# The product of the merged branches as seven products of quarters

## The chip, the cores and the metric

The kernel runs on one core of a Trainium2 chip. The metric is the device time of one launch in microseconds (us), as the median of several runs. Engines are named as the profile names them: PE is TensorE (PEld its weight loads), DVE VectorE, ACT ScalarE, POOL GpSimd, SP the engine that issues most transfers.

## What is computed

Two blocks of a model follow each other on 512 tokens of width 1024, in float32. The change is in the first one:

```python
gates = jax.nn.sigmoid((u @ w_gate[l] + b_gate[l]).astype(jnp.float32)).astype(u.dtype)
g_ssm, g_attn = jnp.split(gates, 2, axis=-1)
merged = g_ssm * (y_ssm @ w_up_ssm[l]) + g_attn * (y_attn @ w_up_attn[l])
h = h + merged @ w_out[l]
hid = jax.nn.relu(rmsnorm(h, norm_mlp[l]) @ w_ff1[l])
h = h + (hid * hid) @ w_ff2[l]
```

`y_ssm` and `y_attn` have width 512, `merged` and `w_out` 1024, `w_ff1` is 1024 x 4096. The product at issue is `merged @ w_out[l]`, 512 x 1024 by 1024 x 1024. Before it stand the two up-projections, behind it the norm and the feed-forward products.

## The kernel before

Every product of float32 numbers is made of three matmuls: both sides are split into a high part and a rest (`split`, L281: ACT copies to the rounded type, DVE subtracts it from the source), and `mm3` (L289) adds high by high, high by low and low by high. Weights come in chunks of 128 x 1024 (0.5 MB). A plan, the list that `order` (L1897) makes, gives their sequence: `load` (L317) fetches a chunk on SP's queue, `chunk_split` (L333) splits it on ACT and DVE, and at most four split pairs live at a time (`PAIRS`); `done` (L352) frees a pair once its matmuls are written down.

The feed-forward products are made already by seven products of quarters in place of eight (`seven_cm` and `seven`, L417; the names P1 to P7 and their sequence in `SEVEN`, L28). Their weight sides are sums of quarters: in `SUMS` (L30) a chunk is either loaded, or a transfer on POOL's queue adds the next quarter to a buffer that holds the one before (`accum_op`, L330). Results of P1, P2 and so on are added to `h` or subtracted from it as they come (`seven_h`, L463). Between P5 and P3 the same PSUM bank goes on being summed, so DVE must have read it in between. `Sides` (L110) holds the seven left sides.

Writing the program down, `Net` keeps an estimated clock: side tasks (`spawn`, L179) are put in between the matmuls when their inputs are thought to be ready (`wait`, `when`, L167), and `until` (L205) goes on when a condition holds. A scheduler then fixes the order on each engine, and each engine works off its own list in that order.

In `first` (L1035) the up-projection of the attention branch (L1217) goes over eight blocks m of 128 columns: 12 matmuls, DVE's product with the gate `gt[m, 1]`, POOL's addition of the other branch (`ptt`, L790), and the split into `mg`, a pair of 128 x 8 x 512. The four loads of `h` follow (`open_h`), since `h` takes the place of the gates. `tm_add` (L1239) makes `merged @ w_out` in two halves of 512 columns: for the first half six of eight steps in k for all four row tiles, and then the last two steps; for the second half tile by tile, and behind each tile `norm_sides` (L528) is spawned, the norm, the transposes by PE and the sides of the first feed-forward product. `ff` (L1267) starts its P1 once the tiles 0 and 1 are through, and P5 once 2 and 3 are.

## Time and profile before

| | |
|---|---|
| time, median of 3 runs | 1383.54 us (1383.09 to 1384.86) |
| the profiled execution | 1383.01 us, span 1381.3 us |
| busy: PE, DVE, ACT, POOL | 1346.5, 966.2, 725.2, 213.0 us |
| mean granted clock of PE | 0.995 |
| up-projections end, out-projection begins | 330.1 us |
| first feed-forward matmul | 378.7 us |

The profile is of one execution; its times count from the span's start. Matmuls are pipelined, so the time from one start to the next is what one costs, not its shown duration. A row of the timeline gives start, duration, engine, line, operation, the tile written and those read, and in brackets the engine's idle time before it and what ended that. Most operations have line L73, the helper that records them; so they are told apart by their tiles.

### The profile page before, as it was taken

How to read it: one execution, taken by the hardware profiler on the slowest of the kernel's cores; microseconds unless marked ns; L12 is line 12 of the kernel's file. 1: busy time of each engine (PE TensorE's matmuls, PEld its weight loads, DVE VectorE, ACT ScalarE, POOL GpSimd, SP SyncE). 2: the span in 40 equal slices, each digit the busy share in tenths (PEclk: the TensorE clock that was granted, in tenths of full speed). 3: DMA queues.
4: the chain of work that ended last, by engine and by line, in shares of the span. 5: the costliest groups of instructions: out<-in, count | busy, mean ns of one | idle time of the engine just before them, and what ended most of it. 6: DMA issues, size and time to landing. Idle time of an engine off the chain costs nothing. (4 is left out here: it accounts for less than half of the span.)

```text
span 1381.3 us, 20776 instructions
## 1 busy us (share of the span) xinstructions
PE 1346.5 (97%) x7914; PEld 1125.3 (81%) x7914; DVE 966.2 (70%) x1795; ACT 725.2 (52%) x1215; POOL 213.0 (15%) x248
## 2 busy tenths in 40 slices
PE   8989999999999999999989999999999999999997
PEld 7778886778798998979867776788898989898886
DVE  8987548874588677686883646544668887878555
ACT  6244347742476574746575422324546675756353
POOL 3155214224011111111210011000000000000000
PEclk9989999999999999999999999999999999999999
DMA  7444331113387778878721311322432222222422
GB/s 276 133 131 133 92 107 47 61 62 107 153 198 163 186 181 202 187 174 204 175 75 61 122 65 41 105 86 92 139 109 85 92 77 77 78 76 70 168 92 76
DMA packets 56883, 164.32 MB, mean 119 GB/s; under 512 B 14048, under 2 KB 15200, under 8 KB 56784
## 3 DMA queue, kind: packets, MB, share of 16 engines
q1 hardware_dynamic: 47568, 129.43, 27.3%
q0 software_dynamic: 9216, 33.56, 13.4%
q8 instruction: 63, 1.03, 0.3%
q14 instruction: 36, 0.29, 0.1%
HBM read 156.15 MB, written 6.82 MB: 118 GB/s over the span
## 5 line engine op out<-in xcount | busy, mean ns | idle before, releaser
L223 PE MATMUL bank<-w_hi,x_h 128*128 128x256 f32 (+1 forms) x744 | 257.3, 346 | 0.0
L223 PE MATMUL bank<-x_h,w_hi 128*128 128x512 f32 (+1 forms) x704 | 249.5, 355 | 7.3 <-ACT w_hi L73 5.3
L223 PE MATMUL bank<-w_hi,x_l 128*128 128x256 f32 (+1 forms) x744 | 248.8, 335 | 1.3 <-DVE x_l L73 1.3
L73 DVE TENSOR_TENSOR w_lo<-w_raw,w_hi 128x1024 fp32r<-128x1024 f32 (+1 forms) x160 | 195.0, 1224 | 76.6 <-ACT w_hi L73 76.0
L223 PE MATMUL bank<-w_lo,x_h 128*128 128x256 f32 (+1 forms) x744 | 248.6, 334 | 0.0
L223 PE MATMUL bank<-x_h,w_lo 128*128 128x512 f32 (+1 forms) x704 | 244.5, 347 | 0.0
L223 PE MATMUL bank<-x_l,w_hi 128*128 128x512 f32 (+1 forms) x704 | 244.4, 347 | 0.0
L73 ACT ACTIVATE w_hi<-w_raw 128x1024 fp32r<-128x1024 f32 (+1 forms) x162 | 167.1, 1035 | 126.4 <-PE bank L223 99.7
L223 PEld LDWEIGHTS bank<-w_hi,x_h 128*128 128x128 f32 x744 | 140.2, 189 | 20.7 <-issue 6.9
L223 PEld LDWEIGHTS bank<-x_h,w_hi 128*128 128x128 f32 x704 | 134.3, 191 | 24.9 <-ACT w_hi L73 5.3
L223 PEld LDWEIGHTS bank<-w_hi,x_l 128*128 128x128 f32 x744 | 140.1, 188 | 16.8 <-DVE x_l L73 1.8
L223 PEld LDWEIGHTS bank<-w_lo,x_h 128*128 128x128 f32 x744 | 140.5, 189 | 14.0 <-issue 0.3
L223 PEld LDWEIGHTS bank<-x_h,w_lo 128*128 128x128 f32 x704 | 134.1, 191 | 16.6 <-DVE w_lo L73 0.2
L223 PEld LDWEIGHTS bank<-x_l,w_hi 128*128 128x128 f32 x704 | 134.4, 191 | 14.9 <-DVE x_l L73 0.5
L73 DVE TENSOR_TENSOR w_lo<-w_a,w_hi 128x1024 fp32r<-128x1024 f32 x64 | 77.4, 1222 | 31.2 <-ACT w_hi L73 31.0
L73 ACT ACTIVATE w_hi<-w_a 128x1024 fp32r<-128x1024 f32 x64 | 67.7, 1060 | 59.9 <-PE bank L223 30.6
L73 POOL DMA_DIRECT2D w_a<-in_w_ff_dram x48 | 41.7, 874 | 220.8 <-DVE w_lo L73 204.4
L73 POOL TENSOR_TENSOR r<-v,pw 128x1 f32<-128x1 f32 x40 | 24.1, 604 | 299.3 <-DVE v L73 296.5
L73 DVE TENSOR_TENSOR h<-h,bank 128x512 f32<-128x512 f32 x80 | 54.4, 682 | 18.3 <-PE bank L223 15.1
L73 ACT ACTIVATE w_hi<-w_b 128x1024 fp32r<-128x1024 f32 x32 | 34.0, 1061 | 45.2 <-PE bank L223 39.3
L73 DVE TENSOR_TENSOR w_lo<-w_b,w_hi 128x1024 fp32r<-128x1024 f32 x32 | 38.6, 1222 | 16.2 <-ACT w_hi L73 16.2
L73 POOL TENSOR_TENSOR kn<-kn,gn 128x256 f32<-128x256 f32 x16 | 12.9, 809 | 237.7 <-ACT q L73 129.0
(427 smaller groups left out, 2798.3 us busy)
## 6 DMA issues: line engine op xcount, KB each, us to landing
w_a<-in_w_ff_dram POOLq DMA_DIRECT2D x48, 512.0 KB, 5.6
w_raw<-in_w_g_dram SPq DMA_DIRECT2D x16, 512.0 KB, 3.7
w_a<-in_w_ff_dram SPq DMA_DIRECT2D x16, 512.0 KB, 4.2
w_b<-in_w_ff_dram SPq DMA_DIRECT2D x16, 512.0 KB, 4.8
w_raw<-in_w_ff_dram SPq DMA_DIRECT2D x16, 512.0 KB, 4.7
w_b<-in_w_ff_dram POOLq DMA_DIRECT2D x16, 512.0 KB, 6.0
w_raw<-in_ple_gate_dram SPq DMA_DIRECT2D x16, 512.0 KB, 3.6
w_raw<-in_f_qk_dram SPq DMA_DIRECT2D x16, 512.0 KB, 3.5
```

The lines of the kernel that those rows point to most:

```text
L73: r = f(*args, **kw)
L223: self.nc.tensor.matmul(out, lhs, rhs, start=start, stop=stop, skip_group_check=more)
```

## The change

- The plan lists `w_out` as seven products: 14 chunks, eight loaded and six added by POOL's transfers, in place of eight. For that `wx`, the pool of the buffers `w_a` and `w_b`, is opened before the up-projection, not after it.
- `mg` becomes a pair of 128 x 7 x 4 x 256: the sides of the seven products, by k block and token half. For blocks 0 to 3 the first half is split at once for P1, and one difference is formed. For blocks 4 to 7 a task, `merged_sides`, forms the other sides from the block and its partner of four before: it splits both halves (P2 and P4), makes three sums and differences of 256 elements, and splits four sides at once (128 x 4 x 256).
- `tm_add` is not called here; `seven` is, with `evac` that updates `h` and spawns `norm_sides` for tiles 0 and 1 behind P6, and for 2 and 3 behind P4. From P2 on all four tasks must have been written down.
- Three of the side pairs of the feed-forward product get their memory only after the out-projection.

```diff
--- before.py
+++ after.py
@@ -323,7 +323,7 @@
         (buf, i), chunk, how = part
         if how == "load":
             tag, bufs = ("w_raw", self.RAW) if buf == "c" else (f"w_{buf}", 2)
-            t = self.parts[buf, i] = (self.wp if buf == "c" else self.wx.pool).tile([P, WC], F32, name=tag, tag=tag, bufs=bufs)
+            t = self.parts[buf, i] = (self.wp if buf == "c" else self.wx).tile([P, WC], F32, name=tag, tag=tag, bufs=bufs)
             self.nc.sync.dma_start(t, self.ins[name][chunk])
         else:
             t = self.parts[buf, i]
@@ -552,6 +552,7 @@
                 nc.scalar.activation(a21, b, AF.Copy)
             else:
                 v.tensor_tensor(s1, b, a21, ALU.subtract)
+                yield lambda: len(sides.pairs) == 7
                 self.split(*[cut(t) for t in sides["P5"]], s1)
                 sides.a22.append((tt, b))
             yield 0
@@ -1206,14 +1207,14 @@
         vx.close()
         yx.close()
         cx = ExitStack()
+        self.wx = self.pool(cx, "wx")
+        self.feed()
         pe = self.pool(cx, "pe")
-        ext = [[pe.tile([P, D], F32R, name=f"x{i}{s}") for s in "hl"] for i in range(3)]
-        xf = [t.rearrange("p k t -> p (k t)") for t in self.x]
-        sides = Sides([[t[:, i * D:i * D + D] for t in xf] for i in range(4)] + ext)
         ez = lambda: pe.tile([P, 4, 256], F32, name="z", tag="z", bufs=4)
-        z = [ez() for _ in range(4)]
         mx = ExitStack()
-        mg = self.pair(self.pool(mx, "mg"), 8, "mg")
+        pm = self.pool(mx, "mg")
+        mg = [pm.tile([P, 7, 4, 256], F32R, name=f"mg{s}") for s in "hl"]
+        up, self.merged, zs = slice(0, 256), 0, []
         for m in range(8):
             if m % 2 == 0:
                 w = self.weights("w_upa", m // 2, 8)
@@ -1223,18 +1224,51 @@
             g = self.gt[m, 1]
             nc.vector.tensor_tensor(g, g, b, ALU.mult)
             self.ptt(g, g, self.gt[m, 0], ALU.add)
-            self.split(mg[0][:, m], mg[1][:, m], g)
+            if m < 4:
+                zs.append(ez())
+                self.split(mg[0][:, 0, m], mg[1][:, 0, m], g[:, up])
+                nc.vector.tensor_tensor(zs[m][:, 0], g[:, up], g[:, 256:], ALU.subtract)
+            else:
+                self.spawn(self.merged_sides(mg, m - 4, g, self.gt[m - 4, 1], zs[m - 4]))
         px.close()
         self.open_h(ins["x"])
-        self.wx = ExitStack()
-        self.wx.pool = self.pool(self.wx, "wx", side="right")
+        xf = [t.rearrange("p k t -> p (k t)") for t in self.x]
+        sides = Sides([[t[:, i * D:i * D + D] for t in xf] for i in range(4)])
+        z = [ez() for _ in range(4)]
         tx = ExitStack()
         pn = self.pool(tx, "pn", side="right")
         g = self.row(pn, "norm_mlp")
 
         self.hold = self.plan.index(next(c for c in self.plan if c[:2] == ("w_ff1", (0, "P5", 0))))
-        th = self.tm_add(mg, "w_out", 0, lambda tt: self.norm_sides(pn, sides, z, self.h[tt], tt, g), mid=lambda: None)
-        self.ff(th, tx, mx, cx, sides, z, ez)
+        th = {}
+
+        def evac(p, s, b):
+            self.seven_h(p, s, b)
+            if p in ("P6", "P4"):
+                tt = s if p == "P6" else 2 + s
+                th[tt] = self.spawn(self.norm_sides(pn, sides, z, self.h[tt], tt, g))
+
+        self.seven("w_out", 0, lambda p, s, k: [t[:, LEFT[p], k, s * P:s * P + P] for t in mg], evac,
+                   lambda p: self.until(lambda: p == "P1" or self.merged == 4))
+        mx.close()
+        px = self.pool(cx, "ext")
+        sides.pairs += [[px.tile([P, 4, 256], F32R, name=f"x{i}{s}") for s in "hl"] for i in range(3)]
+        self.ff([th[tt] for tt in range(NT)], tx, cx, sides, z, ez)
+
+    def merged_sides(self, mg, k, g, g0, z):
+
+        v = self.nc.vector
+        up, lo = slice(0, 256), slice(256, 512)
+        s2, s1, s4 = (z[:, LEFT[p] - 3] for p in ("P6", "P5", "P3"))
+        yield self.when(g)
+        self.split(*[t[:, 1:3, k] for t in mg], g.rearrange("p (a t) -> p a t", a=2))
+        v.tensor_tensor(s1, g[:, lo], g0[:, lo], ALU.subtract)
+        v.scalar_tensor_tensor(s2, s1, -1.0, g0[:, up], ALU.mult, ALU.subtract)
+        v.scalar_tensor_tensor(s4, s2, -1.0, g[:, up], ALU.mult, ALU.subtract)
+        yield self.when(z)
+        self.split(*[t[:, 3:7, k] for t in mg], z)
+        self.merged += 1
+        yield self.wait()
 
     def tm_add(self, x, name, idx, then, before=None, mid=None):
 
@@ -1264,10 +1298,9 @@
         hs = self.h[tt][:, cb * 512:cb * 512 + 512]
         self.nc.vector.tensor_tensor(hs, hs, b, ALU.add)
 
-    def ff(self, th, tx, mx, cx, sides, xz, ez):
+    def ff(self, th, tx, cx, sides, xz, ez):
         nc = self.nc
         v = nc.vector
-        mx.close()
         hx = ExitStack()
         slots = lambda name, n: [[t.tile([P, 4, 256], F32R, name=f"{name}{i}{s}") for s in "hl"]
                                  for t in [self.pool(hx, name)] for i in range(n)]
@@ -1365,7 +1398,6 @@
                     norms[2 + s] = self.spawn(self.two_norms(ez, self.x, 2 + s, *z["g"]))
 
             self.seven("w_ff2", q * 8, lambda p, s, k: [t[:, k, s * P:s * P + P] for t in hid[p]], evac, first)
-        self.wx.close()
         hx.close()
         self.gla(norms, cx)
 
@@ -1905,7 +1937,6 @@
         add("w_qk", *range(8))
         add("w_ups", *range(4))
         add("w_upa", *range(4))
-        add("w_out", *range(8))
 
         def seven(name, base):
             for pr in SEVEN:
@@ -1913,6 +1944,7 @@
                 for i in range(2):
                     p.append((name, (base, pr, i), ((buf, i), base + 4 * c + 2 * k + i, how)))
 
+        seven("w_out", 0)
         for q in range(4):
             seven("w_ff1", 8 * q)
             seven("w_ff2", 8 * q)
```

The order of the instructions moves most on DVE. The first place is the end of the up-projection, from the split of block 5 to the split of block 7 (`gt51`, `gt61`, `gt71` are the gates of blocks 5 to 7, `mg_l` or `mgl` the low sides, `z` the sums and differences). DVE before:

```order
L73 TENSOR_TENSOR mg_l_3142<-gt51_546,mg_h_3141 128x512
L73 TENSOR_TENSOR gt61_544<-gt61_544,bank_3263 128x512
L73 TENSOR_TENSOR mg_l_3142<-gt61_544,mg_h_3141 128x512
L73 TENSOR_TENSOR gt71_542<-gt71_542,bank_3280 128x512
L73 TENSOR_TENSOR w_lo_3294<-w_raw_3177,w_hi_3293 128x1024
L73 TENSOR_TENSOR mg_l_3142<-gt71_542,mg_h_3141 128x512
```

DVE with the change, the same stretch:

```order
L73 TENSOR_TENSOR z_3177<-gt51_546,gt11_554 128x256
L73 TENSOR_TENSOR mgl_3137<-gt51_546,mgh_3136 128x2x256
L73 SCALAR_TENSOR_TENSOR z_3177<-z_3177,gt11_554 128x256
L73 TENSOR_TENSOR mgl_3137<-z_3153,mgh_3136 128x4x256
L73 SCALAR_TENSOR_TENSOR z_3177<-z_3177,gt51_546 128x256
L73 TENSOR_TENSOR gt61_544<-gt61_544,bank_3265 128x512
L73 TENSOR_TENSOR gt71_542<-gt71_542,bank_3287 128x512
L73 TENSOR_TENSOR mgl_3137<-z_3177,mgh_3136 128x4x256
L73 TENSOR_TENSOR w_lo_3303<-w_raw_3128,w_hi_3302 128x1024
L73 TENSOR_TENSOR mgl_3137<-gt61_544,mgh_3136 128x2x256
L73 TENSOR_TENSOR z_3196<-gt61_544,gt21_552 128x256
L73 TENSOR_TENSOR mgl_3137<-gt71_542,mgh_3136 128x2x256
```

The products with the gates of blocks 6 and 7 now stand side by side, behind the sides of blocks 4 and 5, and the low parts of 6 and 7 behind a split of 128 x 4 x 256 and one of weights.

The second place is the passage from P5 to P3 in the out-projection, with the change only. DVE, from the last sides on (`bank_3331` and `bank_3350` are P1's banks, `bank_3383` and `bank_3397` P2's, `bank_3421` and `bank_3435` those of P5 and P3):

```order
L73 TENSOR_TENSOR mgl_3137<-z_3220,mgh_3136 128x4x256
L73 TENSOR_TENSOR w_lo_3412<-w_b_3261,w_hi_3411 128x1024
L73 TENSOR_TENSOR h0_3314<-h0_3314,bank_3331 128x512
L73 TENSOR_TENSOR h1_3315<-h1_3315,bank_3350 128x512
L73 TENSOR_TENSOR h0_3314<-h0_3314,bank_3383 128x512
L73 TENSOR_TENSOR h1_3315<-h1_3315,bank_3397 128x512
L73 TENSOR_TENSOR w_lo_3417<-w_b_3306,w_hi_3416 128x1024
L73 TENSOR_TENSOR h2_3316<-h2_3316,bank_3421 128x512
L73 TENSOR_TENSOR h3_3317<-h3_3317,bank_3435 128x512
```

and PE at the same passage:

```order
L223 MATMUL bank_3435<-w_hi_3376,mgl_3137 128x512
L223 MATMUL bank_3331<-w_hi_3449,mgh_3136 128x512
L223 MATMUL bank_3350<-w_hi_3449,mgh_3136 128x512
L223 MATMUL bank_3421<-w_hi_3411,mgh_3136 128x512
L223 MATMUL bank_3421<-w_lo_3412,mgh_3136 128x512
```

Two matmuls of P6 are put ahead of P3, whose first one writes the bank that DVE reads for `h2`; that reading stands behind four updates of `h0` and `h1` and both splits of P3's weights.

The third place is ACT at the passage from P2 to P5 of the first feed-forward product (`x1h` is the side of P5, made in two parts; `w_hi` are weight splits). Before:

```order
L73 ACTIVATE z_3136<-bank_3737 128x4x128
L73 ACTIVATE w_hi_3799<-w_b_3629 128x1024
L73 ACTIVATE x1h_3130<-z_3137 128x4x128
L73 ACTIVATE x_h_69<-bank_3753 128x4x128
L73 ACTIVATE x_h_69<-z_3136 128x1024
L73 ACTIVATE w_hi_3804<-w_b_3641 128x1024
```

With the change:

```order
L73 ACTIVATE z_3324<-bank_3774 128x4x128
L73 ACTIVATE w_hi_3838<-w_b_3651 128x1024
L73 ACTIVATE x1h_3665<-z_3325 128x4x128
L73 ACTIVATE x_h_69<-bank_3780 128x4x128
L73 ACTIVATE w_hi_3843<-w_b_3657 128x1024
L73 ACTIVATE x1h_3665<-z_3325 128x4x128
```

The second weight split from `w_b`, which stood behind the last part of `x1h`, now stands ahead of it.

## Rows read from the trace of the kernel before

**Rows 1.** The page: busy time of PE, and its granted clock in 40 slices.

```profile
PE 1346.5 (97%) x7914; PEld 1125.3 (81%) x7914; DVE 966.2 (70%) x1795; ACT 725.2 (52%) x1215; POOL 213.0 (15%) x248
...
PEclk9989999999999999999999999999999999999999
```

**Rows 2.** Windows: stretch, length, busy time (count) by engine, clock, DMA share, GB/s.

```profile
330.00:379.00 49.00, 47.95 (x217) 38.28 (x216) 24.88 (x35) 18.16 (x27) 7.80 (x7) 1.00 0.39 151
379.00:401.00 22.00, 19.59 (x159) 18.63 (x157) 19.18 (x23) 14.84 (x19) 6.45 (x8) 1.00 0.89 185
```

**Rows 3.** Timeline of PE, from the out-projection to the first feed-forward matmul.

```profile
330.13 0.40 PE L223 MATMUL bank<-w_hi,mg_h 128*128 128x512 f32 x1
...
354.64 0.40 PE L223 MATMUL bank<-w_hi,mg_h 128*128 128x512 f32 x1
...
357.19 0.50 PE L223 MATMUL bank<-w_hi,mg_h 128*128 128x512 f32 x1 [0.29 <-ACT w_hi L73]
358.45 0.50 PE L223 MATMUL bank<-w_lo,mg_h 128*128 128x512 f32 x1 [0.76 <-DVE w_lo L73]
...
378.74 0.28 PE L223 MATMUL bank<-x_h,w_hi 128*128 128x256 f32 x1
```

**Rows 4.** Timeline of ACT: a high part of `mg`, and the last split of w_out.

```profile
312.90 0.63 ACT L73 ACTIVATE mg_h<-gt 128x512 fp32r<-128x512 f32 x1 [4.04 <-POOL gt L73]
...
356.08 1.06 ACT L73 ACTIVATE w_hi<-w_raw 128x1024 fp32r<-128x1024 f32 x1 [7.88 <-DMA w_raw<-in_w_out_dram]
```

**Rows 5.** Timeline of PE's weight loads, first feed-forward product from P5 on.

```profile
391.76 0.19 PEld L223 LDWEIGHTS bank<-x1h,w_hi 128*128 128x128 f32 x1 [0.36 <-ACT x1h L73]
...
400.26 0.19 PEld L223 LDWEIGHTS bank<-x2h,w_hi 128*128 128x128 f32 x1 [1.37 <-ACT z L73]
400.91 0.19 PEld L223 LDWEIGHTS bank<-x2l,w_hi 128*128 128x128 f32 x1 [0.46 <-DVE x2l L73]
```

**Rows 6.** Timeline of DVE: two instructions over 1024 elements, back to back.

```profile
393.96 1.22 DVE L73 SCALAR_TENSOR_TENSOR z<-z 128x1024 f32<-128x1024 f32 x1
395.10 1.22 DVE L73 TENSOR_TENSOR w_lo<-w_b,w_hi 128x1024 fp32r<-128x1024 f32 x1
```

**Rows 7.** Timeline of DVE in the up-projection: products with the gates, the last low part.

```profile
310.81 0.69 DVE L73 TENSOR_TENSOR gt<-gt,bank 128x512 f32<-128x512 f32 x1 [0.70 <-PE bank L223]
...
314.17 0.68 DVE L73 TENSOR_TENSOR gt<-gt,bank 128x512 f32<-128x512 f32 x1
314.77 1.22 DVE L73 TENSOR_TENSOR w_lo<-w_raw,w_hi 128x1024 fp32r<-128x1024 f32 x1
...
318.44 0.68 DVE L73 TENSOR_TENSOR gt<-gt,bank 128x512 f32<-128x512 f32 x1
...
340.73 0.69 DVE L73 TENSOR_TENSOR mg_l<-gt,mg_h 128x512 fp32r<-128x512 f32 x1 [1.84 <-ACT mg_h L73]
```

**Rows 8.** Groups by form: a DVE subtraction over 256 elements (busy us, mean ns).

```profile
L73 DVE TENSOR_TENSOR l<-kn,k 128x256 fp32r<-128x256 f32 x16 | 6.7, 421 | 1.3 <-ACT k L73 1.2
```

**Rows 9.** Timeline of POOL in the up-projection: additions of blocks 0 and 1.

```profile
311.58 1.29 POOL L73 TENSOR_TENSOR gt<-gt,gt 128x512 f32<-128x512 f32 x1 [18.82 <-DVE gt L73]
314.93 2.21 POOL L73 TENSOR_TENSOR gt<-gt,gt 128x512 f32<-128x512 f32 x1 [2.07 <-DVE gt L73]
```

**Rows 10.** Tile `h`, 341 to 355 us: its four loads, from issue to landing.

```profile
DMA to landing us min/median/max: 3.1/5.1/6.9
```

**Rows 11.** Timeline of DVE: the last updates of `h` for tiles 2 and 3.

```profile
372.45 0.69 DVE L73 TENSOR_TENSOR h<-h,bank 128x512 f32<-128x512 f32 x1
...
380.11 0.68 DVE L73 TENSOR_TENSOR h<-h,bank 128x512 f32<-128x512 f32 x1
```

**Rows 12.** Timeline of PE behind its longest wait for DVE.

```profile
90.96 1.33 PE L228 MATMUL bank<-ident,w 128*128 128x128 f32 x5 [3.54 <-DVE w L73]
```

**Rows 13.** Windows behind that wait; the column after the engines is the granted clock.

```profile
90.00:95.00 5.00, 4.04 (x40) 3.65 (x41) 5.00 (x8) 3.46 (x4) 2.84 (x3) 0.50 0.34 94
95.00:100.00 5.00, 5.00 (x13) 3.86 (x12) 4.96 (x11) 0.42 (x2) 0.77 (x2) 0.51 0.50 167
```

## The prediction, made before the changed kernel ran

> **What bounds the kernel now.** Read the page's busy times first: TensorE (PE) is busy 97% of the span and its granted clock stands at full speed almost throughout [rows 1]. So time is gained by fewer matmuls, and lost wherever PE is made to wait. Then the windows around the changed stage [rows 2]: from 330 to 379 us, the out-projection, PE is busy 47.95 of 49.00 us, DVE only 24.88; from 379 to 401, where the first feed-forward products begin, DVE is already busy 19.18 of 22.00. The timeline of PE gives the price of a matmul and the waits of before [rows 3]: from the first matmul of the out-projection, 330.13, to the 106th, 354.64, lie 105 steps, 0.2334 us each. Then come two gaps. The matmuls at 357.19 and 358.45 wait for the split of the last weight chunk, and ACT had stood 7.88 us for that chunk's transfer [rows 4]. Without them the matmuls after 356.51 would have followed at 0.23 us; they lose 1.6 us together. The first feed-forward matmul starts at 378.74. The weight loads of PE in the next stage show the waits there, the longest 1.37 us [rows 5].
>
> **What the change removes.** The out-projection had 8 x 2 x 4 x 3 = 192 matmuls of 512 columns; seven products of 2 x 4 x 3 make 168. 24 x 0.2334 = **5.6 us** less. The Trainium skill (TensorE: Matmul & The Clock Gate, "Wait — 56ns, not 53.3ns?") states 215.7 ns from start to start at N = 512; by that it would be 5.2, and the row decides. The late chunk goes too: all w_out loads now stand ahead of the loads of h and w_ff1 in SP's queue, and the adding ones on POOL are issued early. That is another 1.6, so **-7.2 us**. The eight groups of transposes are the same, and only change places.
>
> **What it adds, and where it lies.** Splits of weights go from 8 to 14, with six transfers of 0.5 MB more, sides of seven quarters instead of one, and DVE runs all of it in a fixed order. A DVE instruction over 1024 elements takes 1.22 and starts the next after 1.14 [rows 6]; one over 512 after 0.60 (314.17 to 314.77) [rows 7]; one over 256 takes 0.42 [rows 8], so I give it 0.34.
>
> *P2.* Before, a block of the up-projection went through DVE product, POOL add, ACT hi, DVE lo, one after the other: 3.36 us from one product to the next (310.81 to 314.17), 4.27 with a weight split between (314.17 to 318.44) [rows 7]. The POOL add takes 1.29 alone and 2.21 where a 1.22 us DVE split runs beside it [rows 9]: DVE's time nearly all comes on top. The last block's lo was done at 341.4 (340.73 and 0.69), eleven us after PE had left the up-projections; that cost nothing, since PE had 72 matmuls on blocks 0 to 5 to do first. Now PE does P1 (blocks 0 to 3) from 330.1 to 335.7 and P2 at once wants blocks 4 to 7. Walking the new order with the same durations: blocks 0 to 3 get a bit faster (2.9 and 4.1, since their halves are 256 wide), so block 4's product starts at 324.8. Block 4 takes 3.7. Block 5 takes 6.1, as a weight split, a 512 lo, three 256 sides and the 1024 lo of block 4 stand ahead of block 6's product. Blocks 6 and 7 are multiplied at 334.6 and 335.2, but their POOL adds then run beside two 1.2 us DVE instructions and end at 339.1 and 341.3; ACT's hi takes 0.63 [rows 4], and block 7's lo ends at 342.7. P2's first half wants that at 338.2 and so ends 4.4 later. If the adds took 1.29 each it would be 1.5, and 4.9 if both suffered in full. I take **+4.4**.
>
> *P5.* DVE has 342.0 to 348.9 full: the sides of blocks 6 and 7 and both weight splits of P5. PE comes to its last k-step at 348.3: **+0.6** (0 to 1).
>
> *P3.* P3 writes on into the bank of P5, so the subtraction of P5 into h[2] must have read it. That stands seventeenth in a queue that runs unbroken from 342.0: 5 of 0.6, 5 of 0.34, 6 of 1.14 make 11.5, then 0.7 itself, so 354.2; and 0.5 more for the loads of h, which now wait for the last reader of gt (345.5, where they were issued at 341.45) and took 3.1 to 6.9 to land [rows 10]. PE is done with P5, and two matmuls of P6 put ahead, at 352.4: **+2.3** (0 if DVE is ahead, 4 if h[1] lands late).
>
> *P7 and P4.* The norms of rows 0 and 1 start after P6 and stand in DVE's queue between weight splits that must wait for PE to free their buffers. Two transposes wait 0.4 each, and P4 waits 0.8 for the update of h[2], behind two norm products: **+1.6** (0 to 2).
>
> *First feed-forward products.* h[2] and h[3] were final at 373.1 and 380.8, 5.6 before and 2.1 after the first feed-forward matmul [rows 11]; in my walk both are updated about 1 before and 1 after it. In ACT's order the split of a P3 weight chunk, which waits for P2's end, now stands ahead of the last part of P5's side. So P5 starts in full only 2.4 after P2's end, and P3's side is done 10.4 after it, where it was 9.5 (P2's end is 0.36 before the weight load at 391.76, the side was awaited at 400.91) [rows 5]: **+0.9** (-1, if the earlier weight splits relieve DVE there, to +2.5).
>
> Sum: -7.2 + 4.4 + 0.6 + 2.3 + 1.6 + 0.9 = +2.6. The profiled execution took 1383.01, so 1385.6; the median of the runs is 0.5 above it: **1386.1 us**. What comes behind 401 us has the same order on all engines and is counted at nothing; its cover is the unchanged PE load.
>
> **Rivals.** (a) *The sides are in time.* If POOL's adds are not slowed and DVE keeps gaps, the waits fall to 1.5 + 0.3 + 0.8 + 0.5 + 0 and the sum to -4.1: 1379.4. For it: 1.29 us of the adds with DVE idle [rows 9]. Against it: DVE's queue after 334 has no gap to give, and even the bare chain product, add, hi, lo of block 7 ends after PE wants it.
>
> (b) *The clock falls.* Between 337.1 and 342.7 PE would have six matmuls, 1.4 us of work. At 90.96 PE had stood 3.54 us waiting for DVE [rows 12], and in the windows from 90 to 100 its granted clock was 0.50 and 0.51, that is 1.2 GHz [rows 13]. The Trainium skill (TensorE: Matmul & The Clock Gate, "HAM oscillation — how this bites in real kernels") says that such pauses between bursts bring the clock back to half; the trace agrees at that place. Here ten us at half clock would cost 5 us of matmuls, of which the waits at P5 and P3 (2.9) would absorb most, as DVE goes on meanwhile. It decides if the wait at P2 is one long one; my walk breaks it at 339.8, 340.5 and 342.0. Price 2 to 3: 1388.6.
>
> (c) *Late loads.* The four loads of h now share the engines with two adding loads. If h[1] or h[2] lands 3 us later than I put it, it holds all of DVE's queue, the weight splits too: 1389.
>
> **Chances.** A change of 0.2% (2.8 us) is about what a measurement can tell here. My forecast, that the new waits take back a little more than the saving, gets 0.58, with 1383.5 to 1388.5 as its own range: 0.34 within 0.2%, 0.24 slower. It ends near the edge, as the sum is small beside its terms. Rival (a) gets 0.18 (0.16 faster, 0.02 within), (b) 0.14 (0.13 slower), (c) 0.10 (0.08 slower). Together: faster 0.16, within 0.2% 0.39, slower 0.45. The range goes from 1380.5, which takes in part of (a), to 1390, beyond (b) and (c).
>
> **What would show it.** Right: 168 matmuls on mg; a wait of PE for ACT or DVE on mg after the first quarter of P2, 3 to 5 us together; a wait before P3 released by DVE h; POOL's add of block 6 near 3 us long; the first feed-forward matmul at 379 to 381. Wrong: P2 without a wait, or the first feed-forward matmul before 376 (then (a)); a granted clock of 0.5 after 337 (then (b)); DVE standing for a transfer of h (then (c)); or a new wait behind 401, which I have at nothing.

## The result, and the profile after

| | before | with the change |
|---|---|---|
| time, median of 4 runs each | 1384.2 us | 1392.3 us (1391.1 to 1392.8) |
| ratio, 95% interval | | 1.0054 (1.0036 to 1.0071) |
| span of the profiled execution | 1381.3 us | 1390.2 us |
| busy PE, DVE | 1346.5, 966.2 us | 1348.0, 987.9 us |

The change makes the kernel slower by 8.1 us, where 2.6 was forecast; the time lies outside the range of 1380.5 to 1390. One thing ahead is to be set right: the change has six loads and eight adding transfers of w_out, not eight and six. The table `SUMS` in the code says so, and so do the queues on the page of the changed kernel (packets, MB, share of 16 engines):

```profile
q1 hardware_dynamic: 47280, 128.38, 27.8%
q0 software_dynamic: 10368, 37.75, 15.3%
```

Before they moved 129.43 and 33.56 MB: two transfers of 0.52 MB less on the one queue, eight more on the other.

The first matmul on `mg` starts at 329.48, 0.65 earlier than before [rows 3], the first feed-forward matmul at 383.02 and not at 378.74. The timeline of PE (start, duration, operation, idle time before it and what ended that) shows where the out-projection stands:

```profile
336.55 0.50 PE L223 MATMUL bank<-w_hi,mgh 128*128 128x512 f32 x1
339.17 0.50 PE L223 MATMUL bank<-w_lo,mgh 128*128 128x512 f32 x1 [2.12 <-DVE w_lo L73]
340.71 0.50 PE L223 MATMUL bank<-w_hi,mgl 128*128 128x512 f32 x1
341.67 0.63 PE L223 MATMUL bank<-w_hi,mgl 128*128 128x512 f32 x1
...
350.76 0.40 PE L223 MATMUL bank<-w_hi,mgl 128*128 128x512 f32 x1
352.81 0.72 PE L223 MATMUL bank<-w_hi,mgh 128*128 128x512 f32 x2 [1.66 <-ACT w_hi L73]
356.48 0.80 PE L223 MATMUL bank<-w_hi,mgh 128*128 128x512 f32 x1 [2.95 <-DVE h L73]
357.50 0.63 PE L223 MATMUL bank<-w_hi,mgl 128*128 128x512 f32 x1
...
383.02 0.37 PE L223 MATMUL bank<-x_h,w_hi 128*128 128x256 f32 x1
397.99 0.50 PE L223 MATMUL bank<-x1h,w_hi 128*128 128x256 f32 x2 [1.60 <-ACT x1h L73]
```

The wait in P2 is where it was forecast. It is followed by matmuls of 0.63 us instead of 0.40, at half the clock (1.2 of 2.4 GHz). P5 then runs through, and its last matmul is at 350.76. The two matmuls of P6 that stand ahead of P3 wait for a weight, P3 itself for DVE's update of h, and the clock falls again. What DVE waits for there is plain in its timeline:

```profile
347.93 0.68 DVE L73 TENSOR_TENSOR h<-h,bank 128x512 f32<-128x512 f32 x1
351.82 0.69 DVE L73 TENSOR_TENSOR h<-h,bank 128x512 f32<-128x512 f32 x1 [3.21 <-DMA h<-in_x_dram]
353.62 1.22 DVE L73 TENSOR_TENSOR w_lo<-w_b,w_hi 128x1024 fp32r<-128x1024 f32 x1
355.74 0.69 DVE L73 TENSOR_TENSOR h<-h,bank 128x512 f32<-128x512 f32 x1 [0.90 <-DMA h<-in_x_dram]
359.53 0.69 DVE L73 TENSOR_TENSOR h<-h,bank 128x512 f32<-128x512 f32 x1 [3.10 <-DMA h<-in_x_dram]
```

DVE stands 7.2 us for loads of h, in a queue that holds everything else; P3 starts right behind the update at 355.74, ahead of which DVE has stood 4.1 us (3.21 and 0.90). The issues of transfers between 290 and 360 us (count, KB each, median us to landing) and the windows show how slow these loads are:

```profile
w_a<-in_w_out_dram POOLq DMA_DIRECT2D x4, 512.0 KB, 6.8
h<-in_x_dram SPq DMA_DIRECT2D x4, 512.0 KB, 9.6
...
w_b<-in_w_out_dram POOLq DMA_DIRECT2D x2, 512.0 KB, 9.4
```

```profile
340.00:350.00 10.00, 10.00 (x36) 7.71 (x36) 8.61 (x13) 4.73 (x5) 2.60 (x3) 0.83 0.69 184
350.00:360.00 10.00, 5.40 (x15) 3.70 (x15) 4.18 (x6) 2.11 (x2) 0.86 (x1) 0.75 1.05 283
```

Before, the loads of h landed after 3.1 to 6.9 us [rows 10]. Now they are issued at 343.54, behind the last sum that reads a gate. Until their last one has landed, at 359.4, four adding transfers are issued beside them, at 343.44, 344.91, 348.31 and 355.13. The row of the first one shows why they come just then:

```profile
343.44 0.88 POOL L73 DMA_DIRECT2D w_a<-in_w_out_dram  x1 [5.40 <-DVE w_lo L73]
```

It adds to a buffer whose former content DVE had to split first, so it can't go out ahead of that split. All transfer engines are busy from 350 to 360 us (share 1.05), and PE works 5.4 of those 10 us.

To compare kernels whose stages start at different times, I add up, along the timeline of PE from the first matmul on `mg` to the first on `x1h`, what lies between two starts beyond the pitch (0.2334 us for 512 columns, 0.119 for 256). At half the clock the excess is 0.2 us per matmul; that has a column of its own. P6/P3 is all of P3 and, where the order has them (the changed kernel, e1, e4), the two early matmuls of P6 ahead of it.

| excess, us | P1 | P2 | P5 | P6/P3 | rest | x1h | half clock | all | time to x1h |
|---|---|---|---|---|---|---|---|---|---|
| before | 0 | 0 | 0 | 0 | 1.2 | 0.3 | 0 | 1.6 | 61.6 |
| changed | 0 | 3.2 | 0 | 5.4 | 0.1 | 1.75 | 3.6 | 14.0 | 68.5 |
| e1, h early | 0 | 4.35 | 0.1 | 0.9 | 0.1 | 1.8 | 2.3 | 9.5 | 64.0 |
| e2, block order | 1.4 | 0.9 | 0.5 | 3.9 | 2.1 | 1.75 | 0 | 10.7 | 65.1 |
| e3, both | 1.4 | 1.8 | 0.7 | 1.1 | 1.0 | 1.8 | 0 | 7.8 | 62.2 |
| e4, plain loads | 0 | 3.1 | 0.6 | 4.6 | 0.1 | 1.75 | 1.6 | 11.7 | 66.2 |
| e5, e3 and row tiles | 1.4 | 1.8 | 0.7 | 1.1 | 1.4 | 0.6 | 0 | 7.0 | 61.5 |
| e6, e5 and k in halves | 0 | 0.9 | 2.9 | 3.0 | 0.8 | 1.8 | 1.6 | 11.0 | 65.4 |
| e9, e5 and adds on DVE | 1.4 | 0.9 | 0.9 | 1.8 | 1.5 | 0.6 | 0 | 7.0 | 61.5 |
| e12, e9 and late h | 1.4 | 0 | 0.6 | 1.7 | 1.7 | 1.8 | 0 | 7.1 | 61.6 |

The matmuls themselves got 5.6 us less, as forecast, and the excess 12.5 us more: 6.9 us in all. With 0.65 us less ahead of the stage and 2.7 more behind it, that is the 8.9 us by which the span grew.

### The profile page after: what moved, and what is told of

It is laid out like the page before. It is cut to its first block, busy times and chain, and to the rows that moved or that the text cites. A ratio compares the mean times of both kernels' runs of the same rounds, so it can differ in the third digit from the quotient of the medians.

```text
span 1390.2 us, 20802 instructions
## 1 busy us (share of the span) xinstructions
PE 1348.0 (97%) x7890; PEld 1124.0 (81%) x7890; DVE 987.9 (71%) x1827; ACT 735.0 (53%) x1225; POOL 216.9 (16%) x256
## 3 DMA queue, kind: packets, MB, share of 16 engines
q1 hardware_dynamic: 47280, 128.38, 27.8%
q0 software_dynamic: 10368, 37.75, 15.3%
## 4 chain that ended last, share of the span: by engine, by line
PE 74%; DVE 13%; DMA 4%; ACT 4%; issue 3%; POOL 2%; SPq 0%; POOLq 0%; DVEq 0%; ACTq 0%
PE bank L223 70%; PE bank L228 4%; DVE w_lo L73 3%; ACT w_hi L73 2%; DMA w_a<-in_w_ff_dram 2%; DVE u L73 1%; DVE z L73 1%; DVE h L73 1%; DMA h<-in_x_dram 1%; POOL beta L73 1%; DVE l L73 1%; DVE cm L73 1%; POOL gt L73 1%; DVE x_l L73 1%; DVE gt L73 0%
## 5 line engine op out<-in xcount | busy, mean ns | idle before, releaser
L73 DVE TENSOR_TENSOR w_lo<-w_raw,w_hi 128x1024 fp32r<-128x1024 f32 (+1 forms) x154 | 189.0, 1232 | 70.4 <-ACT w_hi L73 69.6
L73 ACT ACTIVATE w_hi<-w_raw 128x1024 fp32r<-128x1024 f32 (+1 forms) x156 | 160.9, 1035 | 116.0 <-PE bank L223 96.8
L73 ACT ACTIVATE w_hi<-w_a 128x1024 fp32r<-128x1024 f32 x72 | 75.8, 1056 | 68.0 <-PE bank L223 31.0
L73 DVE TENSOR_TENSOR w_lo<-w_a,w_hi 128x1024 fp32r<-128x1024 f32 x72 | 88.2, 1238 | 31.6 <-ACT w_hi L73 31.5
L73 DVE TENSOR_TENSOR h<-h,bank 128x512 f32<-128x512 f32 x86 | 58.4, 683 | 22.2 <-PE bank L223 11.6
L73 ACT ACTIVATE w_hi<-w_b 128x1024 fp32r<-128x1024 f32 x36 | 38.1, 1058 | 51.6 <-PE bank L223 48.2
L73 DVE TENSOR_TENSOR w_lo<-w_b,w_hi 128x1024 fp32r<-128x1024 f32 x36 | 43.5, 1223 | 18.8 <-ACT w_hi L73 18.8
```

Source lines behind the costliest of these rows:

```text
L73: r = f(*args, **kw)
```

## The experiments

All change the kernel with seven products. Names in the table are theirs.

**e1.** The gates of one branch lie in the memory of h, and each row tile of h is loaded once its two gates are used up.

```diff
+        ph = self.pool(self.hx, "ph", side="right")
+        self.h = [ph.tile([P, D], F32, name=f"h{tt}") for tt in range(NT)]
...
+        self.pg.update({(m, 0): self.h[i // 2][:, i % 2 * 512:i % 2 * 512 + 512] for i, m in enumerate((0, 1, 2, 3, 4, 5, 6, 7))})
...
             self.ptt(g, g, self.gt[m, 0], ALU.add)
+            if m % 2:
+                i = (0, 1, 2, 3, 4, 5, 6, 7).index(m) // 2
+                nc.sync.dma_start(self.h[i], ins["x"][i])
```

> The gates of one branch are kept in the memory of h, and each h tile is loaded as soon as its two gates are used up, so that the loads of h run during the up-projection, where few transfers are under way. Theory A (late h): in the changed kernel the loads of h are issued only at 343.5 us and share the transfer engines with the adding loads, DVE stands 7.2 us for them in a queue that holds everything else, P3 starts late and the clock falls; what P2 loses is hidden behind that. Then here DVE stands under 1 us for h, the wait before P3 (2.95 us) falls below 1, the first feed-forward matmul comes at 377 to 379.5 us instead of 383.0, and the time is 1385 to 1388.5. Theory B (the sides on DVE are the bound, h only comes last by accident): the wait before P3 stays over 2 us, the first feed-forward matmul comes at 381 or later, and the time is 1390 to 1392.

1387.15 us, ratio 1.0026 (1.0013 to 1.0039). PE's order is the same as in the changed kernel. The loads land after a median of 3.8 us, DVE never stands for h, and P3 comes without a wait of its own; the first feed-forward matmul comes at 377.88. This is PE where it stood for P6 and P3:

```profile
353.26 0.97 PE L223 MATMUL bank<-w_hi,mgh 128*128 128x512 f32 x3 [0.68 <-ACT w_hi L73]
```

The excess at P6/P3 falls from 5.4 to 0.9 us, and P3's matmuls now run at full clock: theory A, and B is out as what holds P3. The wait in P2 gets 1.1 us longer, with 2.3 us of half clock behind it and not 1.5, but the first feed-forward matmul still comes 4.5 us sooner after the first on `mg`: 2.0 of that is P3's earlier start, 2.3 its full clock. So the late loads of h cost 4 to 5 us.

**e2.** The blocks of the up-projection in the order 0, 1, 4, 5, 2, 3, 6, 7.

```diff
-        for m in range(8):
+        for m in (0, 1, 4, 5, 2, 3, 6, 7):
...
-        add("w_upa", *range(4))
+        add("w_upa", 0, 2, 1, 3)
```

> The up-projection goes over the blocks in the order 0, 1, 4, 5, 2, 3, 6, 7, so that the sides of blocks 4 and 5 are made while blocks 2 and 3 are multiplied, and only those of 6 and 7 are left at the end. Both theories: P2 waits under 1 us for its sides instead of 3.1, and keeps the full clock (1.65 us). Theory A (late h): h is still loaded late, so PE only waits longer before P3, and the first feed-forward matmul comes at 380.5 to 383 us, the time at 1389.5 to 1392.5. Theory B (sides): the gain of 4.7 us arrives, first feed-forward matmul at 378 to 379 us, time 1386.5 to 1388.

1387.74 us, 1.0032 (1.0020 to 1.0045); first feed-forward matmul at 379.30: theory B's time, and 0.3 us past its range for the matmul. The wait in P2 fell to 0.9 and the clock stayed up, though P1 now waits 1.4 for the sides of blocks 2 and 3. But the run doesn't separate A and B as meant: with earlier sides the gates were free earlier, h was issued at 341.1 instead of 343.5, landed after 5.7 us, and DVE didn't stand for it. So late sides and late loads are one chain. What is left is the two halves of P3, each of which PE's weight loads await. The first (351.00) starts behind DVE's update of h at 350.21, to which DVE came without a pause. The second (355.45) starts behind the update at 354.71; that one stood on DVE behind the split of a weight of P6, for whose adding transfer ACT had stood 7.77 us:

```profile
350.21 0.68 DVE L73 TENSOR_TENSOR h<-h,bank 128x512 f32<-128x512 f32 x1
351.00 0.19 PEld L223 LDWEIGHTS bank<-w_hi,mgh 128*128 128x128 f32 x1 [2.46 <-issue]
...
352.48 1.06 ACT L73 ACTIVATE w_hi<-w_a 128x1024 fp32r<-128x1024 f32 x1 [7.77 <-DMA w_a<-in_w_out_dram]
353.57 1.23 DVE L73 TENSOR_TENSOR w_lo<-w_a,w_hi 128x1024 fp32r<-128x1024 f32 x1 [2.69 <-ACT w_hi L73]
354.71 0.68 DVE L73 TENSOR_TENSOR h<-h,bank 128x512 f32<-128x512 f32 x1
355.45 0.19 PEld L223 LDWEIGHTS bank<-w_hi,mgh 128*128 128x128 f32 x1 [1.81 <-DVE h L73]
```

**e3.** Both edits.

> Both edits together: h early and the blocks in the order 0, 1, 4, 5, 2, 3, 6, 7. Theory A and theory B both expect no wait over 1 us between P1 and P3, the full clock, and the first feed-forward matmul at 373.5 to 376 us (168 matmuls and the transposes after 329.5 us are 41.4 us, and 2 to 5 us are left for weights that land late and for the norms). If the waits in the first feed-forward product come from the lateness of h, the time is 1379 to 1382; if they are made by the order on ACT and DVE there, about 3 us of them stay and the time is 1382 to 1385, no longer clearly different from the kernel before.

1385.35 us, 1.0013 (1.0002 to 1.0025). In the out-projection no single wait is over 1.1 us and the clock stays up, but 1.4 us in P1, 1.8 in P2, 1.1 before P3 and 1.0 in the rest remain, and the wait for x1h is as long as ever: the second case of the expectation, and 0.4 us above it. The first feed-forward matmul, at 376.85, was 0.85 later than either theory had it.

**e4.** The eight adding transfers become plain ones into the same buffers; the sums of quarters are left out. The order on every engine stays.

```diff
-            self.nc.gpsimd.dma_start(t, self.ins[name][chunk], accum_op=ALU.add)
+            if name == "w_out":
+                self.nc.gpsimd.dma_start(t, self.ins[name][chunk])
+            else:
+                self.nc.gpsimd.dma_start(t, self.ins[name][chunk], accum_op=ALU.add)
```

> The changed kernel, but the eight adding loads of w_out on the POOL queue are plain loads of the same size into the same buffers (the sums of quarters of the weight are left out). Theory A1 (the adding transfers hold the engines and so delay h): h lands after a median of 5 to 6 us instead of 9.6, DVE stands 2 to 4 us for it instead of 7.2, the first feed-forward matmul comes 2 to 4 us earlier. Theory A2 (only the late issue counts): median over 8 us, DVE stands over 6, first feed-forward matmul at 382 or later.

1389.0 us, in a single execution, so that its stages are compared and not its time. DVE stands 3.4 us for h instead of 7.2, and the stage up to the first feed-forward matmul takes 51.20 us instead of 53.54. That is the gain that A1 expects, though only 1.5 us of it is P3's earlier start; most of the rest is fewer matmuls of P3 at half clock. A1's median is not met: h lands after 8.5 us, one load behind the other (4.5, 7.5, 9.6 and 10.8). But what is moved at full use differs. Windows from 350 to 355 us, of the changed kernel and of this one:

```profile
350.00:355.00 5.00, 1.88 (x7) 0.88 (x6) 3.02 (x4) 1.06 (x1) 0.00 (x0) 1.00 1.06 274
```

```profile
350.00:355.00 5.00, 2.11 (x7) 0.94 (x5) 2.71 (x4) 2.12 (x2) 0.00 (x0) 1.00 1.02 414
```

With both at a share of about 1, 414 GB/s go through without adding transfers and 274 with them. An adding transfer holds the engines about twice as long per byte, which the page says too: 15.3% of the span for 37.75 MB against 27.8% for 128.38.

**e5.** As e3, and P7 and P4 of the out-projection go by row tile.

```diff
-        for p in SEVEN:
+        for ps in [(p,) for p in SEVEN if p not in last] + [last] * bool(last):
...
+                todo = [(p, s, range(4)) for s in range(2) for p in ps]
...
-                   lambda p: self.until(lambda: p == "P1" or self.merged == 4))
+                   lambda p: self.until(lambda: p == "P1" or self.merged == 4), last=("P7", "P4"))
```

> As the run with h early and the blocks in the other order, and besides the last two products of the out-projection go by row tile: P7 and P4 for tile 2, then P7 and P4 for tile 3, so that tile 2 of h is final 24 matmuls (5.6 us) before PE leaves the stage, as in the kernel before, instead of 12. In all four kernels with seven products so far PE waited 1.80 us for x1h and 0.70 us for x1l at P5 of the first feed-forward product, whatever came before (0.36 and 1.0 in the kernel before), and lost 1.9 us there against the kernel before. Theory C (the norms of tiles 2 and 3 come too close together at the end): the two waits fall to 0.4 and 1.0 or less, 1.2 to 2 us are won, time 1383 to 1384.3. Theory D (a split of P3's weights on ACT and DVE stands ahead of the side, whenever the norm comes): the waits stay at 1.5 us or more, gain under 0.7 us.

1384.29 us, 1.0001 (0.9991 to 1.0011): level with the kernel before. The wait for x1h, 1.75 us in all kernels with seven products up to here, falls to 0.6, as theory C says; the trace shows that, while the medians of e3 and e5 lie only 1.1 us apart. PE in e3 and in e5:

```profile
391.85 0.50 PE L223 MATMUL bank<-x1h,w_hi 128*128 128x256 f32 x2 [1.60 <-ACT x1h L73]
392.86 0.39 PE L223 MATMUL bank<-x1l,w_hi 128*128 128x256 f32 x1 [0.50 <-DVE x1l L73]
```

```profile
390.06 0.50 PE L223 MATMUL bank<-x1h,w_hi 128*128 128x256 f32 x2 [0.45 <-ACT x1h L73]
391.26 0.38 PE L223 MATMUL bank<-x1l,w_hi 128*128 128x256 f32 x1 [0.70 <-DVE x1l L73]
```

**e6, e7.** As e5, with P1 to P6 of the out-projection in halves of k.

```diff
+            if halves and len(ps) == 1:
+                todo = [(p, s, ks) for ks in ((0, 1), (2, 3)) for s in range(2)]
```

> As the run before this one, and besides the products P1 to P6 of the out-projection go over k in halves: steps 0 and 1 for both row tiles, then steps 2 and 3, so that the sides of the last two blocks and the second weight chunk of a product are wanted 1.4 us later. With both edits before it PE waited 0.79 and 0.94 us in P1, 0.48, 0.42 and 1.34 in P2, 0.65 and 0.37 in P5, 1.26 before P3. Theory E (each wait is a matter of one late piece): the waits in P1 go, those in P2 fall below 1 us together, the stage from the first matmul on mg to the first feed-forward matmul is 43.5 to 45 us instead of 47.2, and the time 1380 to 1382. Theory F (DVE has no time left between 337 and 351 us, where it is busy 13 of 14 us): what is won in P1 and P2 is waited for in P5 and P3, the stage takes 46 to 47 us, the time is within 0.7 us of the run before.

1390.85 us, 1.0049 (1.0035 to 1.0063), 6.6 us more than e5. P1 waits for nothing and P2 0.9, as E says. But PE then waits 2.9 us in P5 and 3.0 before P3, and the clock falls. Theory F has the place, but the loss is far more than its 0.7: both splits of P5's weights now stand on DVE behind the sides.

```profile
342.18 0.68 DVE L73 TENSOR_TENSOR h<-h,bank 128x512 f32<-128x512 f32 x1
342.78 2.35 DVE L73 TENSOR_TENSOR w_lo<-w_a,w_hi 128x1024 fp32r<-128x1024 f32 x2
```

> As the run before this one, with the low part of one weight split (second chunk of P5) on POOL instead of DVE, 1.2 us less for DVE where it is the bound. Theory F expects 0.5 to 1.5 us less than the run before; theory E no change, or 1 us more, if POOL takes over 3 us for that split beside DVE.

1389.44 us, 1.0044 (1.0027 to 1.0060). The edit named an entry that the table isn't asked for, so e7 was the program of e6 in the same order on every engine. It says nothing of F, but it shows that two medians of one program, six executions each, lay 1.4 us apart.

**e9.** As e5, with the gate additions of blocks 6 and 7 on DVE.

```diff
-            self.ptt(g, g, self.gt[m, 0], ALU.add)
+            (nc.vector if m in (6, 7) else nc.gpsimd).tensor_tensor(g, g, self.gt[m, 0], ALU.add)
```

> As e5 (h early, other block order, last two products by row tile), with the additions of the gates of blocks 6 and 7 on DVE instead of POOL. In e3 the two POOL additions took 2.55 us together, DVE stood 0.8 us for the first, and a DVE subtraction of 256 elements beside the second took 1.51 instead of 0.41. On DVE each should take 0.7. Theory F (DVE has no time left there): DVE gets 1.4 us of work and loses 0.8 of standing and 1.1 of slowing, so the waits in P2 (0.47, 0.42 and 1.34 in e5) fall by 0.5 to 1 us, time 1383 to 1384. Theory G (POOL's additions are not what P2 waits for): no change within 0.5 us, or slower.

1384.67 us, 1.0003 (0.9995 to 1.0012): the same as e5, as G has it. P2's wait does fall from 1.8 to 0.9, as F has it, but P6/P3 takes it back (1.1 to 1.8): the time to x1h is 61.5 us in both.

**e10, e11.** The low parts of two weight splits (e10, on e5) or of one (e11, on e9) on POOL.

```diff
-    ON_POOL = {("w_u", 3)}
+    ON_POOL = {("w_u", 3), ('w_out', (0, 'P2', 1)), ('w_out', (0, 'P5', 1))}
...
-        eng = self.nc.gpsimd if self.plan[n] in self.ON_POOL else self.nc.vector
+        eng = self.nc.gpsimd if self.plan[n][:2] in self.ON_POOL else self.nc.vector
```

> As e5, with the low parts of two weight splits (second chunks of P2 and P5) on POOL, 2.4 us less for DVE between 337 and 346 us. (In e7 this was meant for one of them, but the table of exceptions was looked up with another key, so that e7 was the same program as e6.) Theory F: the waits in P2, P5 and before P3 fall by 1.5 to 3 us together, time 1381.5 to 1383. Theory G: the POOL splits take over 2.5 us each and slow DVE beside them, as its additions do, and P2's second chunk is late: no gain, or 1 to 2 us slower.

> As e9, with the low part of the second chunk of P5 on POOL. Theory F: 1 to 2.5 us less than e5, time 1382 to 1383.3. Theory G: within 0.7 us of e5.

1387.01 us, 1.0023 (1.0012 to 1.0033), and 1387.97 us, 1.0034 (1.0021 to 1.0047): both slower than e5. For e10 that is theory G; e11 lies outside what either theory gave, with 2.0 us of excess in P5 and 3.9 at P3. In e10, POOL's two splits, and DVE instructions over 256 elements beside and without them:

```profile
336.31 2.56 POOL L73 TENSOR_TENSOR w_lo<-w_raw,w_hi 128x1024 fp32r<-128x1024 f32 x1
...
344.81 2.68 POOL L73 TENSOR_TENSOR w_lo<-w_a,w_hi 128x1024 fp32r<-128x1024 f32 x1
```

```profile
336.66 2.48 DVE L73 SCALAR_TENSOR_TENSOR z<-z,gt 128x256 f32<-128x256 f32 x1
...
339.67 0.41 DVE L73 SCALAR_TENSOR_TENSOR z<-z,gt 128x256 f32<-128x256 f32 x1
...
344.75 3.03 DVE L73 SCALAR_TENSOR_TENSOR z<-z,gt 128x256 f32<-128x256 f32 x1
```

Of the 2.4 us taken off DVE, 2.07 and 2.62 come back at these two places: 4.7 us.

**e12.** As e9, with the updates of h by P1 and P2 written behind those by P5.

```diff
+            if p in ("P1", "P2"):
+                late.append((p, s, b))
+                return
             self.seven_h(p, s, b)
+            if (p, s) == ("P5", 1):
+                for l in late:
+                    self.seven_h(*l)
```

> As e9, with the four updates of h by P1 and P2 written behind those by P5, so that they no longer stand on DVE ahead of the sides, of P5's weights and of the update that P3 waits for (four times 0.6 us). Theory F (DVE's one queue between 336 and 349 us is what PE waits for in P2, P5 and before P3): the excess of 0.76, 0.57 and 1.02 us at these three places in e9 falls to under 0.8 together, and the time to 1382 to 1383.5, if the transposes keep their places in the feed-forward product. Theory H (PE's waits only move on to the next late thing, P6's weights by adding transfers and the norms): under 0.6 us are won, the excess shows up behind P3, before P6 or P7, or at x1h.

1386.91 us, 1.0018 (1.0009 to 1.0027). P2's wait is gone, P5's a little smaller, P6/P3's the same 1.7 us, and the wait for x1h is back at 1.8, with the transposes at other places in PE's order: theory H.

**e8, e13, e14, e15.** Repeats of the kernel before (e8, e14), the changed one (e13) and e5 (e15), one execution each.

> The kernel before once more, for its stages: how far two profiled executions of one kernel differ. If the drift of 1 to 2 us that the kernels with seven products show against it behind 700 us, where all engines have the same order, is chance, the same marks (first feed-forward matmul, 700 us, end) differ here by 1 us or more; if it belongs to the change, they agree within 0.5 us.

> The changed kernel once more, for the stretch behind the first wait for x2l (408 us), where all engines have the order of the kernel before. It took 982.1 us there, the kernel before 980.4 and 980.2, the other kernels with seven products 980.3 to 984.6. If the change costs something there in itself, this run takes 981.7 to 982.6; if these 2 us are the scatter of executions, it may lie anywhere from 980 to 984.5, over 0.5 us from the first.

> The kernel before a third time, same stretch (980.4 and 980.2 us so far). If its time there is fixed, 980.0 to 980.6; if executions scatter, outside that.

> e5 once more, same stretch: 980.3 us so far, while its other runs had a median 2.8 us above the profiled one. If the stretch scatters, 981 to 984 here; if it is fixed for one program, 980.0 to 980.6.

e13 repeats the changed kernel's stage within 0.1 us: first feed-forward matmul 53.52 us behind the first on `mg` (53.54), first on x1h 68.49 (68.51), 7.5 us of DVE's standing for h (7.2). In the kernel before, the wait for x1h scatters: 0.3, 1.5 and 1.1 us of excess in three executions, so that the change adds 0.3 to 1.4 there. From the first matmul on x2l to the end the kernel before takes 980.4, 980.2 and 980.3 us, the changed one 982.1 and 983.4, e5 980.3 and 981.7, the others with seven products 981.7 to 984.5. So the stretch is fixed before, scatters with the change, and is longer by 2 to 3 us in the changed kernel, although the order of all engines is the same there from 409 us on. One place was seen: near 919 us a 0.5 MB load of `g_out` took 4.1 us to land, where the same load of the kernel before had taken 3.1, and PE's weight load then stood 0.84 us for its split, where it had not waited. In the repeats it took 4.5 us (e13) against 3.2 and 3.4 (e8, e14). Why such transfers come later there stays open.

## Why the prediction was wrong

**The saving held.** 168 matmuls, the same pitch, no late chunk at the end: the -7.2 us are there.

**P2** was rightly placed: forecast a wait of 4.4, found 3.2 of waiting and some 1.5 of half clock behind it. The parts are not right, so that the sum comes out so close is luck: the additions on POOL took 3.51 us together and ended at 338.0, where the walk had 341.3. It was DVE that stood for POOL: the wait ended on the split of P2's own weights, which stands on DVE ahead of the low part of block 6 and took 2.28 us beside POOL's second addition, where such a split took 1.22 [rows 7].

```profile
334.53 3.51 POOL L73 TENSOR_TENSOR gt<-gt,gt 128x512 f32<-128x512 f32 x2 [3.88 <-DVE gt L73]
336.83 2.28 DVE L73 TENSOR_TENSOR w_lo<-w_raw,w_hi 128x1024 fp32r<-128x1024 f32 x1
```

**P5** cost nothing (0.6 forecast), **P7 and P4** 0.1 (1.6 forecast).

**P3 is the step that failed.** Forecast: "0.5 more for the loads of h", 2.3 in all, 4 at most. Measured: DVE stood 4.1 us for h ahead of the update that P3 waits for. That update ended at 356.4, where the walk had 354.7, although DVE's own work was 1.9 us ahead of the walk. PE lost 5.4 us at P6/P3, and some 2 us of half clock behind it. The landing was taken from loads that shared the engines with plain loads alone [rows 10], and only the delay of the issue was added. But the loads came among adding transfers (four, not the two assumed), and landed after 9.6 us in the median. That these would be "issued early" was wrong too: only the first two were out before 330 us, the other six waited for splits on DVE. e1, with PE's order unchanged, gives the loss back (5.4 to 0.9); e4 shows that about half of DVE's standing belongs to the adding transfers (7.2 to 3.4). Of the 5.4 us, 1.9 are the weight of P6, which the walk had in time. It comes by one of the adding transfers, and ACT stood 5.00 us for it.

```profile
351.70 1.06 ACT L73 ACTIVATE w_hi<-w_a 128x1024 fp32r<-128x1024 f32 x1 [5.00 <-DMA w_a<-in_w_out_dram]
```

**The rivals were taken as alternatives, and two came together.** (b), the clock, had 0.14 and a price of 2 to 3. The excess at half clock is 3.6 us, but the 1.5 of it in P2 lie ahead of a wait that DVE ends, so only the 2 in P3 lengthen the stage by themselves. (c), the late loads, had 0.10 and 3; P6/P3 missed its forecast by 3.1. They are not independent: both falls of the clock came behind waits of PE (2.1 us in P2; 1.7 and 2.9 ahead of P3), and the waits of the second were made by the late transfers. With h early (e1) that fall does not come. Forecast, (b) and (c) in sum are 1386.1 + 2.5 + 2.9 = 1391.5, and the range ended at 1390, beyond each of them singly. That this sum is within 1 us of the measured time is partly luck: the 2.7 us lost behind x1h are not in it, and P5, P7 and P4 cost 2.1 less than forecast.

**The feed-forward product**: forecast +0.9, found 0.3 to 1.4 at x1h, within its bounds. The cause that was named, the weight split ahead of x1h on ACT, is about half of it. What ACT copies to x1h was ready at 396.60, and ACT took it at 397.33, behind that split: 0.7 of the 1.6 us of waiting.

```profile
395.92 0.68 DVE L73 TENSOR_TENSOR z<-bank,z 128x512 f32<-128x512 f32 x1
396.37 1.06 ACT L73 ACTIVATE w_hi<-w_b 128x1024 fp32r<-128x1024 f32 x1 [1.22 <-issue]
397.33 0.61 ACT L73 ACTIVATE x1h<-z 128x512 fp32r<-128x512 f32 x1
```

In e5 row tile 2 is final 24 matmuls ahead of the end of the stage and not 12, the split stands behind x1h again, and the wait falls to 0.45 us. Both changed there at once, so the share of the late norm is argued and not measured by itself.

**Behind x1h** nothing more was counted, as the order is the same. The profiled execution lost 2.7 us there: 0.9 up to x2l, where the clock is at half once more, and 1.8 behind that (3.1 in the repeat), for which no cause was found.

No version was found that beats the kernel before. With h early, the other block order and the last products by row tile (e5) the change is worth nothing and costs nothing. What it saves on PE, 5.6 us, is what PE waits in e5 beyond the kernel before (7.0 - 1.6 = 5.4): from 337 to 351 us DVE is busy 13.1 of 14.0 us there, and was 7.5 in the kernel before. Three ways to relieve it (e6, e9, e12) were waited for at the next late piece, and two that used POOL (e10, e11) made the kernel slower. That DVE is the bound there fits all five, but no run gave it free time to show it.

## What to carry to other kernels

Fewer matmuls are worth what the engines that prepare them have to spare in that stage: here DVE went from about half busy to no pause at all from 331.4 to 348.6 us, and the waits that e6, e9 and e12 removed came back one product later. When a change adds transfers, walk the transfer engines as a queue of their own, with the rate that the kind of transfer has, and not a landing time from a stretch without that kind. And when two rivals have a common cause, price them together before the range is drawn.

## What was not expected of the hardware

**An adding transfer takes about twice the engine time per byte.** From the page: 15.3% of 16 engines' span for 37.75 MB, 27.8% for 128.38 MB; that is 1.87 times per byte. e4 tells the adding from the queue: the same bytes on the same queue, eight transfers of it without adding, take 14.5% and not 15.3. With the engines full, the kernel before moved 418 GB/s with plain loads alone, and e1 211 with adding transfers alone; 274 went through in the changed kernel with both.

```profile
350.00:355.00 5.00, 5.00 (x23) 4.04 (x22) 2.03 (x4) 0.00 (x0) 0.00 (x0) 1.00 1.03 418
```

```profile
355.00:360.00 5.00, 5.00 (x23) 4.04 (x22) 2.49 (x3) 2.11 (x3) 1.50 (x2) 1.00 1.07 211
```

**A DVE instruction on two SBUF operands stood still while POOL worked on its own.** In e10 it took 0.41 us alone, 2.48 and 3.03 beside POOL's splits of 2.56 and 2.68, ending 0.3 us after them. The Trainium skill (SBUF — State Buffer, "SBUF: two separate sides") calls the port pair of DVE and GpSimd an exclusive lock, held for a whole instruction; the trace agrees, with these numbers.

**Nearly the same wait did not always bring the clock down.** In the changed kernel PE's weight loads waited in P2 0.34, 2.44, 0.41 and 0.40 us, in e4 0.26, 2.43, 0.41 and 0.40; the granted clock of the next windows was 0.66 in the one, half for some of the time, and 1.00 in the other. The repeat of the changed kernel (e13: 0.34, 2.43, 0.42, 0.41) fell as well, with 0.66 from 338 to 343 us. The changed kernel, and e4:

```profile
340.00:345.00 5.00, 5.00 (x15) 3.67 (x15) 5.00 (x10) 3.15 (x4) 0.97 (x2) 0.66 0.45 123
```

```profile
340.00:345.00 5.00, 4.83 (x19) 3.43 (x20) 5.00 (x11) 3.16 (x4) 0.57 (x1) 1.00 0.34 105
```

What made the difference is not shown, so a fall in such a place can be given a chance beforehand, not a certainty. In P2 it didn't decide: without it, e4 waited for h all the same before P3.
